# A prologue in a written order on three engines: filter network first, transposes of x later, and products of zeros in the gaps

## The chip, the cores and the metric

The kernel runs on one core of one Trainium2 chip. The metric is device time in microseconds from launch to end. Engine names are those of the profile: TensorE (PE; its weight loads PEld), VectorE (DVE), ScalarE (ACT), GpSimd (POOL), SyncE (SP, which here only issues loads).

## The reference

Two layers of a diffusion backbone over 512 tokens of 1024 channels, all in float32. Layer 0 mixes tokens with a Hyena long convolution beside neighbourhood attention, then a ConvFFN; layer 1 is a Conformer convolution and a ConvFFN. Only the start of layer 0 is touched. What it needs:

```python
shift1, scale1, ... = split(silu(c) @ w_mod[0] + b_mod[0])     # and the same for c_ctx
hn = rms_norm(x, g_mix_pre) * (1 + scale1) + shift1
...
def hyena_filters(length, w1, b1, w2, b2, w3, b3, w4, freq):
    ...
    hdn = jnp.sin(freq[0] * (z @ w1 + b1))          # z (512, 33) is a constant, hidden width 64
    hdn = jnp.sin(freq[1] * (hdn @ w2 + b2))
    hdn = jnp.sin(freq[2] * (hdn @ w3 + b3))
    filt = hdn @ w4                                  # (512, 1024)
    return filt[:, :512] * decay, filt[:, 512:] * decay
def bidirectional_fft_conv(v, h_fwd, h_bwd, bias):   # needs the spectrum of the two filters
    ...
```

## The kernel before

The large products of the kernel run on TensorE as three fp32r products of high and low halves: a high half is a cast by ScalarE (`A.copy`), the low half the difference by VectorE. Weights stream in through SP, are split in this way, and TensorE multiplies. Before the first product of the stream (tile `pz`, the input projection) there is a prologue, and the change is in it alone. Its parts:

- **The filter network.** `layer1`, `layer2` and `layer3` are small float32 products on TensorE (tiles `pf`), each followed by `sin_stage`: VectorE scales and range-reduces (tile `sx`: one to three instructions of L662, then L663 and L664), ScalarE takes the sine (L665; tiles `hdn`, `hdn`, then `h`). `w4x` holds w4 with a negated copy (ScalarE, L717), a decay step (GpSimd, L710) and a copy of that (ScalarE, L718).
- **The filters.** `filt("a")` and `filt("b")` multiply `h` by `w4x` in four float32 products each (L743, tiles `pf`), VectorE multiplies by the decay table (L745, `fx`), ScalarE casts the high half (L746, `fah`/`fbh`), VectorE takes the low half (L747, `fal`/`fbl`); at the end ScalarE makes negated copies (L750, `neg`).
- **The tables of the transform.** `tfr` comes by DMA; ScalarE casts it (L727, `TFh`), VectorE takes the low half (L728, `TFl`).
- **x.** For each of four chunks ScalarE sums squares (L408), GpSimd computes the reciprocal root (L401, L403), VectorE scales (L498, tile `junk`). `x_T(kc)` transposes one column block of all four chunks on TensorE (four products with the identity, L705, tile `pt`), and ScalarE copies it out (L706, `xT`).
- **The modulation.** `gemv_k(k, ...)` multiplies 32-column pieces of silu(c) with the loaded `w_mod` (L674, tile `g`, 16 loads `land`), `columns` brings the result into columns (tile `pm`), `modulate` makes the first operand `hT` out of `xT`.
- **The spectra.** `kspec(fc, pr, half)` is 12 products of a table with a filter for each half (tile `pk`): half 0 uses filter a, half 1 filter b.

The order is a string of step names. TensorE follows it; on the other engines the scheduler places the instructions. All tiles in PSUM come from one pool of eight buffers.

```python
    order_pe.enter_context(tc.manual_schedule(engines={mybir.EngineType.PE}))
    for key in "1 x0 x1 2 x2 x3 3 t0 t1 t2 t3 t4 t5 t6 t7 g0 a b g123 k00 k01 g4567 k100 c m k101 k11".split():
        steps[key[0]](*(int(i) for i in key[1:]))
```

SP issues the loads in the order of another string: four chunks of x, two of `tfr`, two of the decay table, 16 of `w_mod`, 512 KB each. The loads share eight queue semaphores, so each load of `w_mod` is issued when the load eight places ahead of it has landed.

Of the kernel before, what the change touches and what calls it, by code (L numbers as in the profile page):

```python
# [235 lines left out]
def backbone_kernel(ctx: ExitStack, tc: tile.TileContext, a, cols, out, dump=None, stop=None, mark=lambda s: None):  # L236
# [18 lines left out]
    def s4(dt=F32, shape=(P, 2, 512), n="s"):  # L255
        return spool.tile(list(shape), dt, name=nm(n), tag="s")
# [7 lines left out]
    def ps(n="ps"):  # L264
        return pspool.tile([P, 512], F32, name=nm(n), tag="ps")
# [10 lines left out]
    def f(ap):  # L276
        return ap.bitcast(F32)
# [35 lines left out]
    def flat(ap, pat):  # L313
        return ap.rearrange(pat)
# [178 lines left out]
    def norm_chunk(hc, halves=1):  # L493
        junk = s4(F32, (P, 1024), "junk")
        cut = [slice(i * (1024 // halves), (i + 1) * (1024 // halves)) for i in range(halves)]
        r = rstd([sumsq(hc[:, sl], junk[:, sl]) for sl in cut])
        for sl in cut:
            V.tensor_scalar(junk[:, sl], hc[:, sl], r, None, op0=ALU.mult)  # L498
        return junk
# [148 lines left out]
            SP.dma_start(r, a["wmod"][i % 2, i // 2])  # L648
            land[i] = r

    for key in "x0 x1 x2 x3 t0 t1 d0 d1 l0 l1 l2 l3 l4 l5 l6 l7 l8 l9 l10 l11 l12 l13 l14 l15".split():
        load_p(key)


# [3 lines left out]
    def sin_stage(src, i, dst, w):  # L658
        x_ = s4(F32, (P, 1024), "sx")
        v, k = x_[:, 0:w], x_[:, 512:512 + w]  # L660
        for s_, r, o in src:
            V.tensor_scalar(v[r, o], s_[r, o], pc("flt", i)[r], turn[r, i:i + 1], op0=ALU.add, op1=ALU.mult)  # L662
        V.tensor_scalar(k, v, MAGIC, None, op0=ALU.add)  # L663
        V.scalar_tensor_tensor(v, k, MAGIC, v, op0=ALU.subtract, op1=ALU.subtract)  # L664
        return A.activation(dst, v, AF.Sin, bias=0.0, scale=-2.0 * PI_F)  # L665
# [28 lines left out]
        sin_stage([(pm, slice(None), slice(0, 256))], 1, h2, 256)  # L694


    def x_norm(c):
        xns[c] = norm_chunk(xc[c])

    def x_T(kc):  # L700
        if kc % 2 == 0:
# [4 lines left out]
        A.copy(strip(xT[kc // 2][:, kc % 2]), nat(pt))  # L706


    def layer3():
        G.tensor_tensor(w4x[64:128, 0:512], w4x[64:128, 0:512], zt[64:128, 512:1024], op=ALU.mult)  # L710
        pm = [ps("pf") for _ in range(2)]
        for i, o, src, ro in ((0, slice(0, 256), slice(0, 256), 0), (1, slice(256, 512), slice(0, 256), 0),
                              (0, slice(0, 255), slice(1, 256), 64), (0, slice(255, 256), slice(255, 256), 64),
                              (1, slice(255, 511), slice(0, 256), 64), (1, slice(511, 512), slice(255, 256), 64)):
            rs = slice(64 * i, 64 * i + 64)
            PE.matmul(pm[i][ro:ro + 64, o], fl[rs, 128:192], h2[rs, src], start=True, stop=True)
        A.mul(w4x[0:64, 512:1024], w4x[0:64, 0:512], -1.0)  # L717
        A.copy(w4x[64:128, 512:1024], w4x[64:128, 0:512])  # L718
        h3s.append(s4(F32, (P, 1024), "h3"))
        sin3 = sin_stage([(pm[0], slice(None), slice(0, 256)), (pm[1], slice(None), slice(256, 512)),  # L720
                          (pm[1], slice(64, 128), slice(255, 256))], 2, h3s[0][:, 0:512], 512)
        G.memset(h3s[0][64:128, 511:512], 0.0)

        for i in range(2):
            hv = flat(TFh[i], "p a b -> p (a b)")
            with tc.issue_after(sin3.ins):
                A.copy(hv, tfr[i])  # L727
            V.tensor_tensor(flat(TFl[i], "p a b -> p (a b)"), tfr[i], f(hv), op=ALU.subtract)  # L728

    def tfs(lo, ch, cs, fc):  # L730
        t_ = (TFl if lo else TFh)[ch // 2]
# [4 lines left out]
    fb = [p8(n="fbh"), p8(n="fbl")]  # L736
    neg = {}

    def filt(key, dst, which):
        for ch in range(4):  # L740
            s0 = 256 * (ch % 2) + ch // 2
            pm = ps("pf")
            PE.matmul(pm, h3s[0][:, s0:s0 + 255:2], w4x[:, which * 512:(which + 1) * 512], start=True, stop=True)  # L743
            X = s4(F32, (P, 1024), "fx")[:, 0:512]
            V.tensor_tensor(X, pm, dec[ch // 2][:, ch % 2], op=ALU.mult)  # L745
            A.copy(dst[0][:, ch], X)  # L746
            V.tensor_tensor(dst[1][:, ch], X, f(dst[0][:, ch]), op=ALU.subtract)  # L747
        for lo in range(2):
            t_ = s4(F32R, n="neg")
            A.mul(t_, f(dst[lo][:, 2:4]), -1.0)  # L750
            neg[(key, lo)] = t_


    K = {}
# [52 lines left out]
    def modulate():  # L807
# [5 lines left out]
        for kc in range(8):  # L813
# [4 lines left out]
            if kc == 1:  # L818
                ws.splits(2)

    steps = {"1": layer1, "2": layer2, "3": layer3, "x": x_norm, "t": x_T, "g": gemv_k, "c": columns, "m": modulate,
             "a": lambda: filt("a", fa, 0), "b": lambda: filt("b", fb, 1), "k": kspec}
# [723 lines left out]
```

## Time and profile before

| | |
|---|---|
| median of 3 runs | 1267.14 us (1264.29 to 1267.49) |
| the profiled execution | 1264.98 us, its span 1263.2 us |
| PE busy | 1239.3 us (98%) |
| DVE busy | 815.2 us (65%) |
| ACT busy | 509.2 us (40%) |
| POOL busy | 89.4 us (7%) |
| mean granted TensorE clock | 0.999 |
| memory traffic | 134 GB/s over the span |

The profiled execution is one of the faster ones: the median lies 2.16 us above it. Span and time differ by 1.78 us, which lies outside the first and the last instruction. The end of a product is modelled in the profile, so a busy TensorE is not one at its peak: the distance between starts says more than the duration.

### The profile page before, as it was taken

What the parts mean: (1) busy time and instruction counts of PE and PEld (TensorE: products, weight loads), DVE (VectorE), ACT (ScalarE), POOL (GpSimd) and SP (SyncE); (2) the same over time, 40 slices, a digit from 0 to 9 for tenths busy, and PEclk for the clock granted to TensorE, in tenths of its full rate; (3) what the DMA queues carried; (4) which work ended last, traced back from release to release, by engine and by line L of the source; (5) the groups of instructions that cost most, each with busy time, mean ns of one, the idle gap of its engine ahead of it and who ended that gap; (6) DMA issues with size and microseconds to landing.
All of it is one profiled execution on the core that took longest, in us unless ns stands there. A gap on an engine that the chain in (4) does not pass through costs nothing.

```text
span 1263.2 us, 15493 instructions
## 1 busy us (share of the span) xinstructions
PE 1239.3 (98%) x6044; PEld 1024.2 (81%) x6044; DVE 815.2 (65%) x1072; ACT 509.2 (40%) x788; POOL 89.4 (7%) x157
## 2 busy tenths in 40 slices
PE   6999999999999999999999999999999999999997
PEld 3688888988898888887888887878988888888886
DVE  4577696876567788778534576686687555566233
ACT  5453333576443332336223442233544333344221
POOL 3110000231200000000000100012100000000001
PEclk9999999999999999999999999999999999999999
DMA  9535434743136577764344331120265233332321
GB/s 351 192 114 170 133 110 142 257 152 128 40 101 216 184 240 245 226 193 146 117 132 135 131 104 55 50 101 1 68 203 178 88 98 100 100 100 90 95 84 66
DMA packets 47865, 171.64 MB, mean 136 GB/s; under 512 B 5741, under 2 KB 5772, under 8 KB 47792
## 3 DMA queue, kind: packets, MB, share of 16 engines
q1 hardware_dynamic: 47428, 169.93, 41.4%
q8 instruction: 47, 0.77, 0.2%
q0 software_dynamic: 176, 0.40, 0.1%
q10 hardware_dynamic: 188, 0.33, 0.1%
q14 instruction: 26, 0.21, 0.1%
HBM read 167.76 MB, written 2.10 MB: 134 GB/s over the span
## 4 chain that ended last, share of the span: by engine, by line
PE 76%; DMA 9%; DVE 9%; ACT 2%; issue 2%; POOL 1%; DVEq 0%; POOLq 0%; ACTq 0%
PE pz L280 11%; PE pz L281 11%; PE pz L282 11%; PE acc L282 8%; PE acc L280 8%; PE acc L281 8%; DMA raw<-in_wup 4%; DMA raw<-in_wcol 4%; DVE w L298 3%; PE pg L280 2%; PE pg L282 2%; PE pg L281 2%; DVE acc L430 2%; DMA raw<-in_wgate 1%; ACT w L297 1%
## 5 line engine op out<-in xcount | busy, mean ns | idle before, releaser
L281 PE MATMUL pz<-hTl,w 128*128 128x512 f32 (+1 forms) x920 | 345.4, 376 | 0.0
L280 PE MATMUL pz<-hTh,w 128*128 128x512 f32 (+1 forms) x920 | 344.6, 377 | 0.5 <-DVE hTh L521 0.5
L282 PE MATMUL pz<-hTh,w 128*128 128x512 f32 (+1 forms) x920 | 345.1, 376 | 0.0
L298 DVE TENSOR_TENSOR w<-raw,w 128x1024 fp32r<-128x1024 f32 x159 | 193.9, 1222 | 199.9 <-ACT w L297 194.0
L297 ACT CAST w<-raw 128x1024 fp32r<-128x1024 f32 x159 | 166.4, 1051 | 331.8 <-PE pz L281 132.0
L282 PEld LDWEIGHTS pz<-hTh,w 128*128 128x128 f32 x920 | 173.8, 189 | 31.4
L281 PEld LDWEIGHTS pz<-hTl,w 128*128 128x128 f32 x920 | 173.8, 189 | 30.0 <-DVE hTl L522 0.4
L280 PEld LDWEIGHTS pz<-hTh,w 128*128 128x128 f32 x920 | 173.0, 189 | 31.0 <-DVE hTh L521 1.0
L430 DVE SCALAR_TENSOR_TENSOR acc<-raw,sc,acc 128x1024 f32<-128x1024 f32 x74 | 95.4, 1289 | 41.4 <-DMA raw<-in_wgate 20.8
L281 PE MATMUL acc<-w,gs 128*128 128x512 f32 x256 | 99.6, 389 | 0.0
L282 PE MATMUL acc<-w,gs 128*128 128x512 f32 x256 | 98.4, 390 | 0.5 <-DVE gs L1317 0.5
L280 PE MATMUL acc<-w,gs 128*128 128x512 f32 x256 | 97.0, 389 | 0.0
L879 ACT ACTIVATE cv<-pz,pk 128x512 f32<-128x512 f32 x88 | 67.6, 772 | 0.7 <-PE pz L282 0.7
L881 DVE SCALAR_TENSOR_TENSOR cv<-pz,pk,cv 128x511 f32<-128x511 f32 x88 | 65.6, 747 | 1.8
L880 DVE SCALAR_TENSOR_TENSOR cv<-pz,pk,cv 128x511 f32<-128x511 f32 x88 | 65.1, 744 | 0.2 <-ACT cv L879 0.2
L1279 ACT ACTIVATE cv<-cv 128x512 f32<-128x512 f32 x44 | 27.7, 629 | 81.6 <-DVE cv L881 81.5
L282 PEld LDWEIGHTS acc<-w,gs 128*128 128x128 f32 x256 | 48.0, 188 | 10.9 <-DVE gs L1317 0.9
L280 PEld LDWEIGHTS acc<-w,gs 128*128 128x128 f32 x256 | 48.1, 188 | 10.1 <-DVE cv L881 0.2
L281 PEld LDWEIGHTS acc<-w,gs 128*128 128x128 f32 x256 | 48.1, 188 | 9.9
L298 DVE TENSOR_TENSOR wk<-raw,wk 128x1024 fp32r<-128x1024 f32 x30 | 37.1, 1245 | 29.0 <-ACT wk L297 28.9
L536 DVE TENSOR_TENSOR py<-acc,gg 128x512 f32<-128x512 f32 x32 | 21.8, 688 | 49.1 <-ACT py L408 49.1
L399 POOL TENSOR_SCALAR t<-t,t 128x1 f32<-128x1 f32 x19 | 7.0, 369 | 636.6 <-ACT py L408 628.1
(327 smaller groups left out, 1934.5 us busy)
## 6 DMA issues: line engine op xcount, KB each, us to landing
raw<-in_wup SPq DMA_DIRECT2D x88, 512.0 KB, 3.6
raw<-in_wcol SPq DMA_DIRECT2D x48, 512.0 KB, 4.6
raw<-in_wdn SPq DMA_DIRECT2D x44, 512.0 KB, 3.6
raw<-in_wgate SPq DMA_DIRECT2D x32, 512.0 KB, 4.4
raw<-in_pw SPq DMA_DIRECT2D x24, 512.0 KB, 3.9
raw<-in_win SPq DMA_DIRECT2D x20, 512.0 KB, 3.5
land<-in_wmod SPq DMA_DIRECT2D x16, 512.0 KB, 10.4
BM<-in_rpb SPq DMA_DIRECT2D x8, 512.0 KB, 3.4
```

Of the source, the lines that this page charges most:

```text
L280: PE.matmul(o, ah, bh, start=start, stop=False)
L281: PE.matmul(o, ah, bl, start=False, stop=False)
L282: PE.matmul(o, al, bh, start=False, stop=stop)
L297: A.copy(hi, r)
L298: V.tensor_tensor(lo, r, f(hi), op=ALU.subtract)
L399: G.tensor_scalar(v, sums[0], sums[1], EPS, op0=ALU.add, op1=ALU.add)
L430: V.scalar_tensor_tensor(acc, rs[k], ck_, init if k == 0 else acc, op0=ALU.mult, op1=ALU.add)
L536: V.tensor_tensor(p_[:, sl], y2[i], gg[:, sl], op=ALU.mult)
L879: A.activation(dst, pz, AF.Identity, bias=pc(bk, i), scale=pc(wk + "1", i))
L880: V.scalar_tensor_tensor(dst[:, 1:w], pz[:, 0:w - 1], pc(wk + "0", i), dst[:, 1:w], op0=ALU.mult, op1=ALU.add)
L881: V.scalar_tensor_tensor(dst[:, 0:w - 1], pz[:, 1:w], pc(wk + "2", i), dst[:, 0:w - 1], op0=ALU.mult, op1=ALU.add)
L1279: A.activation(cv[:, 0], cv[:, 0], AF.Silu, bias=0.0, scale=1.0)
```

## The change

The scheduler no longer places the prologue's instructions on ScalarE and VectorE: up to the end of filter b, the three engines run in the order in which the code is written. The steps are cut into parts for that (sum and scale of x, product, high half and low half of a filter, high and low half of a table). The network comes first, then filter a, then the tables among the transposes of x, then filter b. The gemv of k = 0 is no longer alone: k = 0 to 3 go in one call. The decay table is loaded ahead of `tfr`. Twenty-three products of a 128x128 tile of zeros stand in the network's gaps on TensorE; nothing reads their result.

```diff
+    warm = cpool.tile([P, P], F32, name="warm")
+    V.memset(warm, 0.0)
+    warm_ps = pspool.tile([P, 512], F32, name="warm_ps", tag="ps")
+    def warm_up(n):
+        for _ in range(n):
+            PE.matmul(warm_ps[:, 0:P], warm, warm, start=True, stop=True)
...
-    for key in "x0 x1 x2 x3 t0 t1 d0 d1 l0 l1 ...".split():
+    for key in "x0 x1 x2 x3 d0 d1 t0 t1 l0 l1 ...".split():
...
-    def x_norm(c):
-        xns[c] = norm_chunk(xc[c])
+    def x_sum(c):
+        xns[c] = s4(F32, (P, 1024), "xn")
+        xns[c, "r"] = rstd([sumsq(xc[c], xns[c])])
+    def x_scale(c):
+        V.tensor_scalar(xns[c], xc[c], xns[c, "r"], None, op0=ALU.mult)
...
+    def filt(key, ch, part):
+        dst, which = (fa, 0) if key == "a" else (fb, 1)
+        if part == "p":
...
+            PE.matmul(fx[key, ch], h3s[0][:, s0:s0 + 255:2], w4x[:, which * 512:(which + 1) * 512], start=True, stop=True)
+        elif part == "m":
...
+            V.tensor_tensor(X, fx[key, ch], dec[ch // 2][:, ch % 2], op=ALU.mult)
+            A.copy(dst[0][:, ch], X)
...
+        else:
+            V.tensor_tensor(dst[1][:, ch], fx.pop((key, ch)), f(dst[0][:, ch]), op=ALU.subtract)
...
+    early.enter_context(tc.manual_schedule(engines={mybir.EngineType.PE, mybir.EngineType.Activation,
+                                                    mybir.EngineType.DVE}))
+    warm_up(5)
+    layer1()
+    warm_up(3)
+    w4_decay()
+    w4_neg()
+    x_sum(0)
+    layer2()
+    warm_up(5)
+    x_sum(1)
+    x_scale(0)
+    layer3(0)
+    warm_up(10)
+    w4_copy()
+    x_sum(2)
+    x_sum(3)
+    layer3(1)
+    for ch in range(4):
+        filt("a", ch, "p")
...
+    for i in range(2):
+        x_T(i)
+        table_hi(i)
+        table_lo(i)
+    for i in range(2, 4):
+        x_T(i)
+    for ch in range(4):
+        filt("b", ch, "p")
+        filt("b", ch, "m")
+        if ch:
+            filt("b", ch - 1, "l")
+    filt("b", 3, "l")
+    early.close()
...
-    for key in "1 x0 x1 2 x2 x3 3 t0 t1 t2 t3 t4 t5 t6 t7 g0 a b g123 k00 k01 g4567 k100 c m k101 k11".split():
-        steps[key[0]](*(int(i) for i in key[1:]))
+    kspec(0, 0, 0)
+    x_T(4)
+    x_T(5)
...
+    kspec(1, 0, 0)
+    x_T(6)
+    x_T(7)
...
+    kspec(0, 0, 1)
+    kspec(1, 0, 1)
+    gemv_k(0, 1, 2, 3)
+    gemv_k(4, 5, 6, 7)
+    kspec(0, 1, 0)
+    columns()
+    modulate()
+    kspec(0, 1, 1)
+    kspec(1, 1)
```

Lines of the changed kernel lie 9 to 92 further down than those of before. From the second filter's end on, every engine has the same instructions in the same order as before, except for the moved transposes and gemv on TensorE, the moved copies and negations of these parts on ScalarE, and one copy of `columns` on VectorE that trades places with its neighbour.

ScalarE before, in the network's stretch (`junk` out of `xc` is a chunk's sum of squares, `hdn` and `h` the sines):

```order
L717 ACTIVATE w4x_80<-w4x_80 64x512
L372 CAST onesr<-ones 128x128
L387 COPY SCT_117<-sc 128x8
L392 ACTIVATE SCT_117<-pk 128x8
L718 COPY w4x_80<-w4x_80 64x512
L665 ACTIVATE hdn_180<-sx_190 128x256
L408 ACTIVATE junk_195,t_196<-xc_84 128x1024
L408 ACTIVATE junk_203,t_204<-xc_85 128x1024
L408 ACTIVATE junk_219,t_220<-xc_86 128x1024
L665 ACTIVATE hdn_180<-sx_214 128x256
L408 ACTIVATE junk_227,t_228<-xc_87 128x1024
L665 ACTIVATE h_59_246<-sx_247 128x512
```

ScalarE in the changed kernel, from the copy for silu(c_ctx) on:

```order
L401 ACTIVATE SCT_120<-pk 128x8
L674 ACTIVATE hdn_183<-sx_198 128x256
L723 ACTIVATE w4x_83<-w4x_83 64x512
L417 ACTIVATE xn_208,t_209<-xc_87 128x1024
L674 ACTIVATE hdn_183<-sx_218 128x256
L417 ACTIVATE xn_228,t_229<-xc_88 128x1024
L729 COPY w4x_83<-w4x_83 64x512
L417 ACTIVATE xn_255,t_256<-xc_89 128x1024
L417 ACTIVATE xn_262,t_263<-xc_90 128x1024
L674 ACTIVATE h_59_269<-sx_270 128x512
```

The first sine has moved ahead of the two `w4x` instructions; the second and the third sine each have as many sums of x ahead of them as the rows show, the last one all four.

VectorE before, from the second sine's range reduction on (L498 scales a chunk of x):

```order
L662 TENSOR_SCALAR sx_214<-pf_211,pk,turn 128x256
L498 TENSOR_SCALAR junk_195<-xc_84,t_200 128x1024
L663 TENSOR_SCALAR sx_214<-sx_214 128x256
L664 SCALAR_TENSOR_TENSOR sx_214<-sx_214 128x256
L498 TENSOR_SCALAR junk_203<-xc_85,t_208 128x1024
L498 TENSOR_SCALAR junk_219<-xc_86,t_224 128x1024
L498 TENSOR_SCALAR junk_227<-xc_87,t_232 128x1024
L662 TENSOR_SCALAR sx_247<-pf_236,pk,turn 128x256
L662 TENSOR_SCALAR sx_247<-pf_237,pk,turn 128x256
L662 TENSOR_SCALAR sx_247<-pf_237,pk,turn 64x1
L663 TENSOR_SCALAR sx_247<-sx_247 128x512
L664 SCALAR_TENSOR_TENSOR sx_247<-sx_247 128x512
```

VectorE in the changed kernel, from the same place:

```order
L671 TENSOR_SCALAR sx_218<-pf_215,pk,turn 128x256
L672 TENSOR_SCALAR sx_218<-sx_218 128x256
L673 SCALAR_TENSOR_TENSOR sx_218<-sx_218 128x256
L711 TENSOR_SCALAR xn_208<-xc_87,t_213 128x1024
L671 TENSOR_SCALAR sx_270<-pf_236,pk,turn 128x256
L671 TENSOR_SCALAR sx_270<-pf_237,pk,turn 128x256
L671 TENSOR_SCALAR sx_270<-pf_237,pk,turn 64x1
L672 TENSOR_SCALAR sx_270<-sx_270 128x512
L673 SCALAR_TENSOR_TENSOR sx_270<-sx_270 128x512
L711 TENSOR_SCALAR xn_228<-xc_88,t_233 128x1024
L711 TENSOR_SCALAR xn_255<-xc_89,t_260 128x1024
L774 TENSOR_TENSOR fx_288<-pf_278,dec_139 128x512
```

Of the four scales of x that stood ahead of the third sine's instructions, one is left; the others follow them, two ahead of the first filter product's `fx`.

TensorE before, from the last transposes on (`g` is the gemv of k = 0, `pf` filter a):

```order
L705 MATMUL pt_305<-ident,junk_219 128x128
L705 MATMUL pt_305<-ident,junk_227 128x128
L674 MATMUL g_311<-land_146,SCT_117 32x512
L674 MATMUL g_313<-land_146,SCT_117 32x512
L674 MATMUL g_315<-land_148,SCT_117 32x512
L674 MATMUL g_317<-land_148,SCT_117 32x512
L743 MATMUL pf_319<-w4x_80,h_59_246 128x512
L743 MATMUL pf_325<-w4x_80,h_59_246 128x512
L743 MATMUL pf_331<-w4x_80,h_59_246 128x512
L743 MATMUL pf_337<-w4x_80,h_59_246 128x512
```

TensorE in the changed kernel, after the third layer, and then the start of the gemv:

```order
L355 MATMUL warm_ps<-warm 128x128 x10
L771 MATMUL pf_278<-w4x_83,h_59_269 128x512
L771 MATMUL pf_280<-w4x_83,h_59_269 128x512
L771 MATMUL pf_282<-w4x_83,h_59_269 128x512
L771 MATMUL pf_284<-w4x_83,h_59_269 128x512
L718 MATMUL pt_306<-ident,xn_208 128x128
L718 MATMUL pt_306<-ident,xn_228 128x128
L718 MATMUL pt_306<-ident,xn_255 128x128
L718 MATMUL pt_306<-ident,xn_262 128x128
```

```order
L683 MATMUL g_460<-land_149,SCT_120 32x512
L683 MATMUL g_460<-land_153,SCT_120 32x512
L683 MATMUL g_460<-land_157,SCT_120 32x512
L683 MATMUL g_460<-land_161,SCT_120 32x512
L683 MATMUL g_465<-land_149,SCT_120 32x512
L683 MATMUL g_465<-land_153,SCT_120 32x512
```

Filter a now comes ahead of the transposes (16 of 32 follow it, the others stand between spectra), and the gemv goes through four different loads, k = 0 to 3, for each of its four results.

## Rows read from the trace of the kernel before

**Rows 1.** Busy time by stretch, TensorE: microseconds, PE busy (records), PEclk, DMA share, GB/s.

```profile
0.00:16.59 16.59, 4.58 (x24) 1.00 0.88 295
...
36.17:47.27 11.10, 11.10 (x51) 1.00 0.11 45
...
63.64:1255.00 1191.36, 1185.84 (x5794) 1.00 0.40 129
```

**Rows 2.** Chain that ended last, first 64 us: start, microseconds, what.

```profile
8.03 0.61 ACT w4x L718
8.67 0.42 ACT hdn L665
...
15.78 0.76 DVE junk L498
16.59 5.46 PE pt L705 x29
22.05 3.55 PE g L674 x8
25.60 7.07 PE pf L743 x16
32.67 3.56 PE g L674 x24
...
47.34 3.57 PE g L674 x32
...
53.86 1.75 PE pm L792 x16
...
63.80 0.26 PE pz L280
```

**Rows 3.** VectorE in order of time: start, microseconds, instruction.

```profile
5.23 0.54 DVE L662 TENSOR_SCALAR sx<-pf,pk,turn 128x256 f32<-128x256 f32 x1
...
6.14 0.43 DVE L664 SCALAR_TENSOR_TENSOR sx<-sx 128x256 f32<-128x256 f32 x1
10.33 0.55 DVE L662 TENSOR_SCALAR sx<-pf,pk,turn 128x256 f32<-128x256 f32 x1 [3.77 <-PE pf L693]
11.22 0.75 DVE L498 TENSOR_SCALAR junk<-xc,t 128x1024 f32<-128x1024 f32 x1 [0.34 <-POOL t L403]
...
16.45 1.31 DVE L662 TENSOR_SCALAR sx<-pf,pk,turn 128x256 f32<-128x256 f32 x3
...
18.25 0.69 DVE L664 SCALAR_TENSOR_TENSOR sx<-sx 128x512 f32<-128x512 f32 x1
```

**Rows 4.** TensorE in order of time, the network's second and third layer.

```profile
9.14 1.12 PE L693 MATMUL pf<-hdn,fl 64*64 64x256 f32 x4 [5.05 <-ACT hdn L665]
13.16 1.25 PE L716 MATMUL pf<-hdn,fl 64*64 64x256 f32 x12 [2.91 <-ACT hdn L665]
```

**Rows 5.** Busy time of transposes alone in a stretch: PE, PEld, DVE, ACT, PEclk, DMA, GB/s.

```profile
16.58:20.69 4.11, 4.10 (x19) 4.11 (x20) 0.00 (x0) 0.24 (x1) 1.00 1.02 417
```

**Rows 6.** SP in order of time, two stretches: issues that wait for x.

```profile
8.53 0.55 SPq L648 DMA_DIRECT2D land<-in_wmod  x1
...
12.58 0.33 SPq L648 DMA_DIRECT2D land<-in_wmod  x1
```

**Rows 7.** Groups of ScalarE by form, 0 to 45 us: count, busy, mean ns.

```profile
L408 ACT ACTIVATE junk<-xc 128x1024 f32<-128x1024 f32 x4 | 4.2, 1044 | 0.0
L706 ACT COPY xT<-pt 128x512 f32<-128x512 f32 x8 | 4.1, 612 | 0.0
L746 ACT CAST fah<-fx 128x512 fp32r<-128x512 f32 x4 | 2.5, 619 | 3.4 <-DVE fx L745 3.4
...
L727 ACT CAST TFh<-tfr 128x1024 fp32r<-128x1024 f32 x2 | 2.1, 1052 | 0.0
...
L665 ACT ACTIVATE h<-sx 128x512 f32<-128x512 f32 x1 | 0.6, 630 | 4.8 <-DVE sx L664 4.8
```

**Rows 8.** Group of VectorE by form, 0 to 45 us: the tables' low halves.

```profile
L728 DVE TENSOR_TENSOR TFl<-tfr,TFh 128x1024 fp32r<-128x1024 f32 x2 | 2.5, 1225 | 3.3 <-ACT TFh L727 3.3
```

More of the change, by code (lines that the diff above doesn't have):

```diff
@@ L649, in load_p @@
             land[i] = r
[L651 removed]
+    for key in "x0 x1 x2 x3 d0 d1 t0 t1 l0 l1 l2 l3 l4 l5 l6 l7 l8 l9 l10 l11 l12 l13 l14 l15".split():
         load_p(key)
@@ L706, in x_T, with w4_neg, w4_decay, w4_copy @@
         A.copy(strip(xT[kc // 2][:, kc % 2]), nat(pt))
-    def layer3():
+    def w4_neg():
+        A.mul(w4x[0:64, 512:1024], w4x[0:64, 0:512], -1.0)
+    def w4_decay():
         G.tensor_tensor(w4x[64:128, 0:512], w4x[64:128, 0:512], zt[64:128, 512:1024], op=ALU.mult)
[L711 to L717, printed above, removed]
-        A.copy(w4x[64:128, 512:1024], w4x[64:128, 0:512])
+    def w4_copy():
+        A.copy(w4x[64:128, 512:1024], w4x[64:128, 0:512])
@@ new lines, in layer3 @@
+    def layer3(part):
+        if part == 0:
+            pm = [ps("pf") for _ in range(2)]
+            h3s.append(pm)
+            for i, o, src, ro in ((0, slice(0, 256), slice(0, 256), 0), (1, slice(256, 512), slice(0, 256), 0),
+                                  (0, slice(0, 255), slice(1, 256), 64), (0, slice(255, 256), slice(255, 256), 64),
+                                  (1, slice(255, 511), slice(0, 256), 64), (1, slice(511, 512), slice(255, 256), 64)):
+                rs = slice(64 * i, 64 * i + 64)
+                PE.matmul(pm[i][ro:ro + 64, o], fl[rs, 128:192], h2[rs, src], start=True, stop=True)
+            return
+        pm = h3s.pop()
@@ L719, in layer3, with table_hi @@
         h3s.append(s4(F32, (P, 1024), "h3"))
-        sin3 = sin_stage([(pm[0], slice(None), slice(0, 256)), (pm[1], slice(None), slice(256, 512)),
-                          (pm[1], slice(64, 128), slice(255, 256))], 2, h3s[0][:, 0:512], 512)
+        sin_stage([(pm[0], slice(None), slice(0, 256)), (pm[1], slice(None), slice(256, 512)),
+                   (pm[1], slice(64, 128), slice(255, 256))], 2, h3s[0][:, 0:512], 512)
         G.memset(h3s[0][64:128, 511:512], 0.0)
[L724 to L728, printed above, removed]
+    def table_hi(i):
+        A.copy(flat(TFh[i], "p a b -> p (a b)"), tfr[i])
@@ L730, in tfs, with table_lo @@
+    def table_lo(i):
+        V.tensor_tensor(flat(TFl[i], "p a b -> p (a b)"), tfr[i], f(flat(TFh[i], "p a b -> p (a b)")), op=ALU.subtract)
     def tfs(lo, ch, cs, fc):
@@ L819, in modulate @@
                 ws.splits(2)
[L821 to L822 removed]
+    early = ExitStack()
+    early.enter_context(tc.manual_schedule(engines={mybir.EngineType.PE, mybir.EngineType.Activation,
[18 more added lines that the diff above has]
+        filt("a", ch, "p")
+    x_scale(1)
+    x_scale(2)
+    filt("a", 0, "m")
+    filt("a", 1, "m")
+    x_scale(3)
+    filt("a", 0, "l")
+    for ch in (2, 3):
+        filt("a", ch, "m")
+        filt("a", ch - 1, "l")
+    filt("a", 3, "l")
+    for i in range(2):
[11 more added lines that the diff above has]
+    early.close()
     order_pe = ExitStack()
     order_pe.enter_context(tc.manual_schedule(engines={mybir.EngineType.PE}))
[L825 to L826 removed]
+    kspec(0, 0, 0)
+    x_T(4)
+    x_T(5)
+    for lo in range(2):
+        negate("a", lo)
+    kspec(1, 0, 0)
+    x_T(6)
+    x_T(7)
+    for lo in range(2):
+        negate("b", lo)
+    kspec(0, 0, 1)
[7 more added lines that the diff above has]
+    kspec(1, 1)
     order_pe.close()
```

17 lines of the change are left out of this document (7 added, 10 removed).

## Prediction

> **What bounds the kernel now.** First the busy time by stretch: from 63.64 to 1255 us TensorE works 1185.84 of 1191.36 us, before 16.59 us it works only 4.58 [rows 1]. So TensorE bounds everything behind the prologue, and since the order there does not change, that part should move as one block: what the prologue gives, the end gives. Then the chain of waits of the first 64 us [rows 2]. It has two parts. Up to 16.59 it lies on ScalarE, GpSimd and VectorE: the first sine (8.67) waits in ScalarE's queue behind the copy into `w4x` (8.03), and at the end the last scale of x (15.78) releases the transposes. From 16.59 on it lies on TensorE alone, without a gap, to the first product of the stream at 63.80: 29 transposes 5.46, gemv of k = 0 3.55, filters 7.07, gemv of k = 1 to 3 3.56, four half spectra (36.23 to 47.34) 11.11, gemv of k = 4 to 7 3.57, a half spectrum 2.95, `columns` 1.75, three half spectra 8.19; together 47.2. So three things can move the end: when TensorE's unbroken work starts, what it contains, and how fast it runs.
>
> As to how fast: the granted-clock column says 1.00 from the start, also where TensorE has not begun, so I go by the pace. Between 16.58 and 20.69 us 19 transposes took 4.10 us, 0.216 each [rows 5]; the 16 of `columns` took 1.75, 0.109 each [rows 2]. That is the ratio of the lower level (1.2 GHz) to the upper (2.4 GHz). 29 at 0.109 are 3.16, with a switch of about 0.2 to the gemv 3.36: about 2.1 us of the 5.46 is the lower level. It ended near 20.8, while TensorE did nothing but transposes: the ten left after 20.69 fit into 1.3 us.
>
> **The change, step by step: when filter a can start.** The first sine's range reduction stays at 5.23 to 6.57 [rows 3]. The sine no longer stands behind the `w4x` copy, so it runs at 6.6 instead of 8.67 and takes 0.42 [rows 2]. The second layer follows at 7.1; VectorE got its result 1.19 after its start [rows 3, 4], so 8.3. The range reduction took 1.34 the first time; the second time, from 10.33, a scale of x (11.22, 0.75) stood in the middle [rows 3]. That scale now comes later, so it ends at 9.65. ScalarE does the sum of chunk 0 ahead of the second sine. x0 had landed by 8.53 (SP's issue of the first `w_mod` load waits for it) [rows 6], a sum takes 1.04 [rows 7], so it is done at about 9.65 too, and the sine ends at 10.1. Third layer from 10.15 to 11.4 [rows 4]. VectorE does one scale in front: chunk 0's sum starts at 8.55 instead of behind the first sine (8.67 + 0.42), 0.55 earlier, so its scale runs from 10.7 to 11.45 instead of 11.22; then the third range reduction, 16.45 to 18.94 before, 2.49 [rows 3]: 11.65 to 14.15. ScalarE meanwhile does three sums and a copy, 3 x 1.04 + 0.61 from 10.1, to 13.85; x3 has landed by 12.58 [rows 6], which leaves the last sum at 12.8 to 13.85. Third sine 0.63 [rows 7]: to 14.8. Filter a at 14.9, where before the filters started at 25.60 and the unbroken work at 16.59.
>
> **What it contains then.** The same pieces by the same rows: filters 7.07, 32 transposes at 0.109 = 3.49, two gemv calls of 3.57, half spectra 11.11 + 2.95 + 8.19, `columns` 1.75: 41.7 us. The gemv of k = 0 alone costs no less than one of three or of four values of k (8, 24 and 32 records in 3.55, 3.56 and 3.57 [rows 2]): the 32-column pieces run beside each other. Two calls of four instead of one, three and four are 3.55 less. All 32 transposes are inside now, where three had run before 16.59, which costs 0.33. There are about four more switches between kinds of work; by the 0.1 to 0.2 that a switch costs in these rows, 0.5. 14.9 + 41.7 + 0.5 = 57.1.
>
> **Does VectorE and ScalarE's part arrive in time?** Filter a's first result reaches VectorE about 1.2 later (as in the second layer [rows 3, 4]): 16.1. From there the two engines alternate over four chunks; with fx and low half at 0.6 to 0.7 (half of the 1.23 of a low half of twice the size [rows 8]), a scale of 0.75 [rows 3] and casts of 0.62 [rows 7], the last low half of filter a is done at 22.2. ScalarE copies a transposed block, casts a table, copies, casts: 0.51 (4.1 for eight) + 1.05 twice [rows 7], from 21.5 to 24.6. VectorE's low halves of the tables take 1.23 each [rows 8]: 23.1 to 24.35 and 24.65 to 25.9. TensorE does filter a to 18.5, four transpose blocks to 20.3, filter b to 23.9, and the first half spectrum wants the first low table at 24.5 and the second at 25.85. That is 0.05 late, on the edge: each microsecond that this alternation takes longer is one that TensorE waits. The eight PSUM buffers go round in order, and filter b's third and fourth product wait for `fx` of chunks 2 and 3 (19.6 and 20.9, wanted at 22.1 and 23.0). Filter b's last low half comes at 33.0, behind two negations that I put at a table cast's 1.05 each; it is wanted at 33.9. All `w_mod` is on the chip by about 37.5: in 36.17 to 47.27 the DMA engines are busy for 0.11 of 11.1 us [rows 1]; the second gemv call would start at 40.1. `modulate` keeps its distance to `columns`, and of the loads behind x3, which land 1.35 apart ((12.58 - 8.53) / 3 [rows 6]), the decay halves come at 13.9 and 15.3, wanted at 16.1 and 19, the tables at 16.6 and 18.0, wanted at 22. I add 0.1: 57.2.
>
> **The products of zeros.** A float32 product is two records; at 128 columns it costs twice a transpose, 0.43 at the lower level, 0.22 at the upper, by rows 5 and 2. Five ahead of the first layer (2.2) end when its data lands, near 3, and VectorE starts at 5.23 anyway. Three fit into the gap before 7.1. Five behind the second layer end at 10.4 at the lower level: third layer 0.2 late. Ten behind the third layer end at 13.8 at the upper, 15.9 at the lower level, against 14.9: 0 to 1.0 late. With layer 2 and the zeros TensorE works unbroken from 7.1 on, and unbroken work came ahead of the rise before; I take the level as up during the ten, so nothing for the zeros, and 1.2 as the bound.
>
> So 63.8 becomes 57.2: a gain of 6.6 us (1.7 earlier start, 3.55 gemv, 2.0 transposes, less 0.6). The sum is made against the profiled execution: 1264.98 - 6.6 = 1258.4; against the median, 1260.5. I give the middle, **1259.4 us**. A change under 0.3%, 3.8 us, is about what a measurement of this kernel cannot tell from none.
>
> In this execution the lower level held until about 20.7 [rows 5], which is 2.1 us of the sum. The Trainium skill (TensorE: Matmul & The Clock Gate, Part 1, "What's actually happening") says of such a ramp that it differs from run to run and warns against fitting to one count. By that rule another execution of the kernel before may have paid less, and the gain against it would be as low as 4.5; by the row it is 6.6. One execution cannot show which.
>
> **Rivals.** *The level rises late.* It may stay down through the zeros and rise only under filter a. Then the ten zeros run to 15.9, and filter a starts there; a record costs 0.88 instead of 0.44 (7.07 / 16) until the rise. None to all eight records so are 0 to 3.5 us; I take five, 2.2, with the late start 3.2. Gain 3.4: 1261.6 on the profiled time, 1262.6 in the middle. For it: layers 1 to 3 did not lift the level before; but they were four microseconds apart (9.14 and 13.16 [rows 4]). *The alternation is slower.* Some ten hand-overs between VectorE and ScalarE lie between 16.1 and 25.9; at 0.1 to 0.2 us more each, TensorE waits 1 to 2 us at the first spectrum: gain 5.1, 1260.9 in the middle. For it: the margin is nil; against: where they alternated before, the rows already hold it. *Slower than before:* the lower level lasts through filters, transposes and first spectra, between which TensorE now changes eight times. Each microsecond of it costs a half, so 6.6 is used up when the low level lasts 13.2 us past 14.9, to 28.1, and the kernel is 0.3% slower when it lasts to 36 (1269 to 1270). Against it: it rose before while the same transposes ran [rows 2, 5]. *The gain is given back later:* no load or engine after 63.64 waits for a fixed moment; TensorE's 5.5 us of idle there are waits for VectorE and ScalarE that move along.
>
> **How the numbers follow.** Forecast 0.64 (its own range 1257 to 1261.5), late level 0.15, slower alternation 0.14, slower than before 0.04, given back 0.03. Faster by over 0.3%: the forecast, the alternation and a third of the late level, 0.64 + 0.13 + 0.05 = 0.82; within: 0.14; slower: 0.04. Range: 1256 if the start falls with the fastest runs (1264.29 - 6.6 = 1257.7, less 1.2 for a faster network at the upper level), to 1263.5, the late level on a slower run.
>
> **What would show it.** Right: first sine near 6.6, third near 14.2; filter a at about 14.9; one gemv of 32 records where two stood; transposes at 0.109; first `pz` near 57. Wrong: transposes or filter products at twice their pace; a wait of TensorE on `TFl` of over 0.5 us; a sine that waits for a sum; `pz` at the old distance from `columns` no longer kept.

## The result, and the profile after

The changed kernel takes 1259.41 us (median of 7 runs, 1257.72 to 1260.61), the kernel before beside it 1266.87 us (7 runs, 1262.99 to 1270.05): a ratio of 0.9947 with a 95% interval of 0.9929 to 0.9965, so it is faster by 0.5%. The forecast was 1259.4 us. The profiled execution of the changed kernel took 1260.43 us, its span 1258.6 us.

The chain that ended last, first 64 us, of the changed kernel (start, microseconds, what):

```profile
4.14 4.87 DMA xc<-in_x
9.04 1.15 ACT xn L417 x2
10.19 0.30 ACT hdn L674
...
13.88 1.27 POOL t L412
15.21 3.68 PE pf L771 x8
18.89 1.75 PE pt L718 x16
20.64 3.44 PE pf L771 x8
...
26.98 0.87 PE pt L718 x8
30.61 0.88 PE pt L718 x8
36.97 7.00 PE g L683 x64
46.92 1.75 PE pm L824 x16
56.84 0.26 PE pz L280
```

These rows answer to [rows 2]. TensorE's unbroken part begins at 15.21 (before 16.59) and is 41.63 long (before 47.21): 16 transposes now take 1.75 and two pieces of eight 0.87 and 0.88, where 29 took 5.46 in one piece, and one piece of 64 `g` products takes 7.00 where three took 10.68 together. The first `pz` stands at 56.84 where it stood at 63.80: 6.96 earlier.

TensorE in order of time, the same stretch (in brackets the idle time before, and what ended it):

```profile
6.64 1.43 PE L702 MATMUL pf<-hdn,fl 64*64 64x256 f32 x4 [0.47 <-ACT hdn L674]
8.00 2.50 PE L355 MATMUL warm_ps<-warm 128*128 128x128 f32 x10
10.54 1.25 PE L740 MATMUL pf<-hdn,fl 64*64 64x256 f32 x12
11.73 2.96 PE L355 MATMUL warm_ps<-warm 128*128 128x128 f32 x20
15.21 3.68 PE L771 MATMUL pf<-w4x,h 128*128 128x512 f32 x8 [0.52 <-POOL t L412]
18.73 1.91 PE L718 MATMUL pt<-ident,xn 128*128 128x128 f32 x16
```

The last group of zeros ends before filter a's operand is there; TensorE then waits 0.52. (The profile puts this down to GpSimd's `t`; ScalarE's sine `h` ends at 15.11, below, and that is what the product reads.) The level of the clock is read from the pace, here by stretch for `warm_ps` alone (PE busy and records, PEld, PEclk, DMA share, GB/s):

```profile
11.73:12.66 0.93, 0.93 (x4) 0.93 (x5) 1.00 1.04 401
12.80:14.40 1.60, 1.60 (x16) 1.60 (x16) 1.00 1.01 369
```

Four records in 0.93, then sixteen in 1.60. The edges of the stretches blur this; the starts of the records lie 0.21 apart up to 12.74 and 0.11 from there on, so the second pace is about twice the first. The trace's own record of the granted clock, which the views do not print step by step, has the rise to the upper level at 12.73 us, within the ten zeros; before, it stood at 20.89, within the transposes. As before, the column prints 1.00 for both stretches.

ScalarE and VectorE in order of time, changed kernel:

```profile
6.17 0.42 ACT L674 ACTIVATE hdn<-sx 128x256 f32<-128x256 f32 x1 [0.81 <-DVE sx L673]
9.04 1.06 ACT L417 ACTIVATE xn<-xc 128x1024 f32<-128x1024 f32 x1 [1.93 <-DMA xc<-in_x]
10.09 0.40 ACT L674 ACTIVATE hdn<-sx 128x256 f32<-128x256 f32 x1
...
14.48 0.63 ACT L674 ACTIVATE h<-sx 128x512 f32<-128x512 f32 x1
```

```profile
13.76 0.69 DVE L673 SCALAR_TENSOR_TENSOR sx<-sx 128x512 f32<-128x512 f32 x1
...
24.51 1.22 DVE L753 TENSOR_TENSOR TFl<-tfr,TFh 128x1024 fp32r<-128x1024 f32 x1 [0.21 <-ACT TFh L750]
```

The first sine no longer stands behind the copy into `w4x` (6.17 instead of 8.67), the second waits for chunk 0's sum, which itself waited 1.93 for the load, the third runs at 14.48. The second low half of the tables is done at 25.73.

### The profile page after: what moved, and what is told of

The parts are those of the page before. It is cut to its first block, busy times and chain, and to the rows that moved or that the text cites. A ratio compares the mean times of both kernels' runs of the same rounds, so it can differ in the third digit from the quotient of the medians.

```text
span 1258.6 us, 15586 instructions
## 1 busy us (share of the span) xinstructions
PE 1243.5 (99%) x6090; PEld 1029.6 (82%) x6090; DVE 815.7 (65%) x1073; ACT 508.7 (40%) x788; POOL 89.2 (7%) x157
## 4 chain that ended last, share of the span: by engine, by line
PE 91%; DVE 3%; DMA 2%; ACT 2%; issue 1%; POOL 0%; SPq 0%; DVEq 0%; POOLq 0%; ACTq 0%
PE pz L280 15%; PE pz L281 15%; PE pz L282 15%; PE acc L282 8%; PE acc L280 8%; PE acc L281 8%; PE pg L280 2%; PE pg L281 2%; PE pg L282 2%; DMA raw<-in_wcol 1%; PE po L1266 1%; PE pt L1246 1%; PE va L280 1%; PE va L281 1%; PE va L282 1%
```

## The experiments

Eleven more kernels were run: ten edits, and the changed kernel a second time. One theory was on trial in all of them: the end moves by as much as the first `pz`, and that is set by the network's start, the contents of TensorE's queue, and the level of the clock. The rivals were that the written order itself is worth nothing (the gemv alone explains it), and that the zeros do nothing.

### Without the products of zeros

```diff
-        for _ in range(n):
+        for _ in range(0):
             PE.matmul(warm_ps[:, 0:P], warm, warm, start=True, stop=True)
```

> The changed kernel without its 23 products of zeros; the output is unaffected. If the zeros are what brings TensorE to its upper level ahead of filter a (in the changed kernel the pace doubled at 12.7 us, inside the ten zeros), then filter a starts at about 15.2 as before but at 0.86 a record instead of 0.43 for most of its eight records, the rise comes inside the filters or the transposes, and the first product of the stream moves from 56.7 to between 58.5 and 60; time 2 to 3.3 us longer. If the level rises by itself with the network's layers, the first product stays at 56.3 to 56.8 and the time is the same.

Measured: 0.9962 of before (0.9952 to 0.9972), first `pz` 59.37 (start of its first record; 56.68 in the change, 63.64 before). TensorE in order of time:

```profile
10.74 1.25 PE L740 MATMUL pf<-hdn,fl 64*64 64x256 f32 x12 [2.74 <-ACT hdn L674]
15.41 6.33 PE L771 MATMUL pf<-w4x,h 128*128 128x512 f32 x8 [3.41 <-POOL t L412]
21.58 1.91 PE L718 MATMUL pt<-ident,xn 128*128 128x128 f32 x16
```

Filter a starts only 0.20 later than in the change (x0 landed that much later: its sum starts at 9.24 instead of 9.04), but its eight records take 6.33 instead of 3.68. The rise is recorded at 20.77, inside filter a. So in this pair of traces the zeros are worth 2.7 us of `pz`, by the level: the one row of filter a has 2.65 of it. The times of the two overlap; the trace is what shows it. It is one pair, and the rise moves from trace to trace: against the next experiment, where it comes at 16.33, the zeros are worth about 1.5 (59.37 - (59.64 - 1.74)), with x0 0.34 later there than here.

### The gemv in three calls again

```diff
-    gemv_k(0, 1, 2, 3)
+    gemv_k(0)
+    gemv_k(1, 2, 3)
```

> The changed kernel with the gemv of k = 0 alone again, then k = 1 to 3, then k = 4 to 7: the work of before in the changed order. If the calls cost by their loads beside each other and not by their number of k, one more call is 3.55 us of TensorE with nothing beside it, and the first product of the stream goes from 56.7 to 60.2, the time up by 3.5. If the gemv of k = 0 is a filler that hides in a wait, or if modulation is waited for anyway, the first product stays within 0.5 us of 56.7.

Measured: 0.9964 (0.9951 to 0.9978), `pz` 59.64. The chain of this kernel, and below it TensorE in order of time:

```profile
38.18 8.74 PE g L683 x64
```

```profile
12.27 4.42 PE L355 MATMUL warm_ps<-warm 128*128 128x128 f32 x20
16.52 3.60 PE L771 MATMUL pf<-w4x,h 128*128 128x512 f32 x8
```

The expectation missed: 1.74 more than 7.00, not 3.5. The starts of the records show why. `gemv_k(0)` has eight records in one 32-column place; four start one after another, 0.43 apart, and the other four each together with three of the next call. In the kernel before, where filter a stood behind it, the same call took its full 3.55. The remaining 1.2 of `pz` is no matter of the gemv: here the rise is recorded at 16.33, the ten zeros last 4.42 instead of 2.96 and filter a starts at 16.52. Up to there the program is the change's own, so this is also a further execution of its start.

### Before, with k = 0 to 3 in one call

```diff
-    for key in "1 x0 x1 2 x2 x3 3 t0 t1 t2 t3 t4 t5 t6 t7 g0 a b g123 k00 k01 g4567 k100 c m k101 k11".split():
+    for key in "1 x0 x1 2 x2 x3 3 t0 t1 t2 t3 t4 t5 t6 t7 a b g0123 k00 k01 g4567 k100 c m k101 k11".split():
```

> The kernel before with only the gemv changed: k = 0 to 3 in one call behind the filters. The sum says 3.55 us less between the transposes and the first spectrum, the first product of the stream from 63.6 to 60.1, the time 3.5 us down, half of the whole gain. The rival, in which the gemv of k = 0 covered a wait for the filter network (its sine was done at 19.6, the transposes at 22), says 63.6, no change.

Measured: 0.9978 (0.9968 to 0.9987), `pz` 60.03, 3.61 earlier than before. In the chain one piece of 32 records stands where 8 and 24 stood:

```profile
29.07 3.57 PE g L674 x32
```

This one edit, without any written order on the other engines, gives half of the move of `pz`: the 3.55 of the prediction.

### Before, with products of zeros

```diff
-    for key in "1 x0 x1 2 x2 x3 3 t0 t1 t2 t3 t4 t5 t6 t7 g0 a b g123 k00 k01 g4567 k100 c m k101 k11".split():
+    for key in "1 w10 x0 x1 2 w6 x2 x3 3 w6 t0 t1 t2 t3 t4 t5 t6 t7 g0 a b g123 k00 k01 g4567 k100 c m k101 k11".split():
```

> The kernel before with 22 products of zeros in TensorE's gaps (ten behind the first layer, six behind the second, six behind the third). If the lower level in the transposes cost 2.1 us, the 29 transposes from 16.6 on now go at 0.109 from the start and the first product of the stream comes at 61.5 instead of 63.6; the six behind the third layer may delay the first three transposes without harm. If zeros do not lift the level, transposes stay at 0.216 until about 20.8 and the first product at 63.6. In time, 2 us or nothing.

Measured: 0.9999 (0.9989 to 1.001), `pz` 62.02. TensorE in order of time:

```profile
4.02 3.94 PE L354 MATMUL warm_ps<-warm 128*128 128x128 f32 x20
8.92 0.65 PE L701 MATMUL pf<-hdn,fl 64*64 64x256 f32 x4 [0.97 <-ACT hdn L673]
...
12.94 0.74 PE L724 MATMUL pf<-hdn,fl 64*64 64x256 f32 x12 [1.84 <-ACT hdn L673]
13.61 2.71 PE L354 MATMUL warm_ps<-warm 128*128 128x128 f32 x12
```

The level rose at 7.06, during the first zeros (`w10` is ten of them), but TensorE then idled for 1.0 and 1.8 us ahead of the second and third layer, the level fell at 13.89, during the last zeros, and rose again at 17.30, during the transposes. `pz` gained 1.62, and the time shows none of it. That the waits left between the zeros are why the level fell is the likely reading; no run tests it.

### The order written for TensorE alone

```diff
-    early.enter_context(tc.manual_schedule(engines={mybir.EngineType.PE, mybir.EngineType.Activation,
-                                                    mybir.EngineType.DVE}))
+    early.enter_context(tc.manual_schedule(engines={mybir.EngineType.PE}))
```

> The changed kernel with the written order on TensorE alone; ScalarE and VectorE are placed by the scheduler again. If the written order on those two is what brings filter a to 15.2 us (sines not behind sums and scales of x), the third sine is late again, filter a starts at 17 to 20 and the first product of the stream comes at 58.5 to 61.5. If the order on TensorE alone does it (network and filters ahead of the transposes), it stays at 56.5 to 57.5, or 58 with a late rise of the clock.

Measured: 1.0065 (1.0045 to 1.0086), slower than before, `pz` 71.52. The size was far off: 14.8 us later than in the change. ScalarE in order of time:

```profile
8.07 0.61 ACT L729 COPY w4x<-w4x 64x512 f32<-64x512 f32 x1 [1.10 <-POOL w4x L726]
17.84 1.04 ACT L750 CAST TFh<-tfr 128x1024 fp32r<-128x1024 f32 x1 [9.15 <-DMA tfr<-in_tf]
18.79 0.41 ACT L674 ACTIVATE hdn<-sx 128x256 f32<-128x256 f32 x1
```

The scheduler put the cast of a table ahead of the first sine. ScalarE waits 9.15 us for the table's load while `sx` has been ready since 6.3; the whole network stands behind it, and the third sine runs at 29.45.

This is not the scheduling of the kernel before. There the casts were tied behind the third sine by one line, which the change dropped:

```diff
-        for i in range(2):
-            hv = flat(TFh[i], "p a b -> p (a b)")
-            with tc.issue_after(sin3.ins):
-                A.copy(hv, tfr[i])
...
+    def table_hi(i):
+        A.copy(flat(TFh[i], "p a b -> p (a b)"), tfr[i])
```

ScalarE before, in order of time:

```profile
18.98 0.63 ACT L665 ACTIVATE h<-sx 128x512 f32<-128x512 f32 x1 [4.83 <-DVE sx L664]
19.52 1.03 ACT L727 CAST TFh<-tfr 128x1024 fp32r<-128x1024 f32 x1
```

So the 14.8 us are the price of giving up the written order without putting that line back. What the scheduler would do in the changed kernel with the line was not run.

### The order written for TensorE and ScalarE

```diff
-    early.enter_context(tc.manual_schedule(engines={mybir.EngineType.PE, mybir.EngineType.Activation,
-                                                    mybir.EngineType.DVE}))
+    early.enter_context(tc.manual_schedule(engines={mybir.EngineType.PE, mybir.EngineType.Activation}))
```

> TensorE and ScalarE in the written order, VectorE in the scheduler's. If ScalarE's queue alone made the kernel with both engines left to the scheduler slow (its first sine stood behind a cast of a table, which waited for the table to land), this one costs only what VectorE's rows cost: the scale of chunk 1 ahead of the third range reduction and those of chunks 2 and 3 in the midst of it, 0.75 us each, and the wait of chunk 3's scale for its sum: third sine 1 to 2.5 us later than in the change, pz 57.8 to 59.3, time 1260 to 1262. If VectorE's order is as costly as ScalarE's, pz is past 62 and the time 1265 or more.

Measured: 0.9987 (0.9974 to 1.0), `pz` 61.69. ScalarE's order was indeed what cost most in the experiment above, but `pz` is 2.4 past the upper end of what was expected, and the time, 1264.3 us, 2.3 past it. TensorE in order of time, and below it by stretch over all engines (span, then PE, PEld, DVE, ACT, POOL, PEclk, DMA share, GB/s):

```profile
11.35 2.50 PE L355 MATMUL warm_ps<-warm 128*128 128x128 f32 x20
17.75 5.28 PE L771 MATMUL pf<-w4x,h 128*128 128x512 f32 x8 [3.90 <-issue]
...
30.80 0.50 PE L282 MATMUL pk<-fah,TFl 128*128 128x512 f32 x1 [0.76 <-DVE TFl L753]
```

```profile
17.75:20.90 3.15, 3.15 (x4) 1.48 (x5) 0.69 (x1) 0.34 (x1) 0.09 (x1) 0.50 1.03 421
21.10:22.80 1.70, 1.70 (x5) 0.73 (x4) 1.59 (x3) 0.34 (x2) 0.00 (x0) 1.00 1.02 412
```

The third sine came 2.54 later (17.02), at the upper end of what was expected: three scales of x stood ahead of it on VectorE. But the zeros had ended, TensorE idled 3.90 us, and the level, up since 10.75, fell at 17.58. The column shows it here: 0.50, then 1.00 from 20.99 on. Filter a's eight records took 5.28, 1.60 more than in the change, and then a table's low half, which VectorE had put behind three `fx`, was 0.76 late. 2.54 + 1.60 + 0.76 are 4.90 of the 5.01 by which `pz` is later. This is the lower level of the prediction's rivals, reached by a late operand.

### The transposes ahead of filter a

```diff
+    for i in range(8):
+        x_T(i)
...
     for ch in range(4):
         filt("a", ch, "p")
```

> The changed kernel with all 32 transposes ahead of filter a, and the three scales of x ahead of filter a's VectorE work; all else as in the change. By the sum nothing but the start of unbroken work changes: it waits for the scale of the last chunk, 16.7 instead of 15.2, so the first product of the stream comes 1.5 later, 58.2. The rival, that filters first is what lets VectorE and ScalarE finish in time, says that TensorE then also waits for the filters' halves or the tables at the first spectrum, 59.5 or later.

Measured: 0.9963 (0.9951 to 0.9975), `pz` 59.05, 2.37 later than in the change. TensorE in order of time:

```profile
15.98 0.38 PE L718 MATMUL pt<-ident,xn 128*128 128x128 f32 x2
16.64 0.33 PE L718 MATMUL pt<-ident,xn 128*128 128x128 f32 x1 [0.27 <-DVE xn L711]
18.15 3.39 PE L718 MATMUL pt<-ident,xn 128*128 128x128 f32 x29 [1.19 <-DVE xn L711]
```

(The edit also puts the scales of x and the casts and low halves of the tables ahead of filter a's work on VectorE and ScalarE; TensorE has no wait for them in this trace.) The fourth transpose needs the last chunk, whose sum, root and scale end at 18.1; filter a needs only the third sine, which ends at 15.75 here. TensorE's unbroken part starts 2.94 later, with 0.33 of transposes already done. The expectation, 58.2, missed by 0.85, and most of that is no matter of the order: x0's sum starts at 9.68 here, 0.64 later than in the change, because the load landed later. About 1.7 of the 2.37 are left for the order. So the network ahead of x counts beside the gemv and the level; the trace shows it, while the interval of the time overlaps that of the change.

### Ten of the twenty-three zeros

```diff
-    warm_up(5)
     layer1()
-    warm_up(3)
...
     layer2()
-    warm_up(5)
```

> The changed kernel with only the ten zeros behind the third layer; the thirteen ahead of it are left out. If the early ones matter, the upper level comes later than at 12.7 or 16.3 us (the two starts seen with all zeros), the ten run at the lower level to about 16.1, and filter a starts 0.9 later and partly at half pace: first product of the stream at 58 to 59.5. If the ten alone are enough, it comes at 56.5 to 58, as with all of them.

Measured: 0.9968 (0.9954 to 0.9982), `pz` 56.82. The rise is recorded at 13.85 instead of 12.73, still within the ten zeros, and `pz` is the change's to 0.14:

```profile
11.86 3.43 PE L355 MATMUL warm_ps<-warm 128*128 128x128 f32 x20
```

The ten last 0.47 longer than in the change, and filter a follows them at 15.35 without a wait. So the thirteen zeros ahead of the third layer gain nothing in this trace. Whether they bring the rise forward it cannot say: in two traces with all of them (11.20 in the second one of the change, 10.75 with TensorE and ScalarE in order) the level rose in the third layer, before the first of the ten.

### The sums of x later, two versions

The first (four zeros follow the second layer instead of five, and the scale of chunk 0 goes behind filter a's products):

```diff
-    x_sum(0)
     layer2()
+    x_sum(0)
     x_sum(1)
...
     x_sum(2)
-    x_sum(3)
     layer3(1)
+    x_sum(3)
```

> The changed kernel with the sum of chunk 0 behind the second sine, the sum of chunk 3 behind the third sine, the scale of chunk 0 behind the third range reduction, and one zero less. In the changed kernel's trace the second sine waited 0.65 us for the sum of x0. If that is what sets filter a, the second sine comes at 9.5 instead of 10.1, filter a at 14.4 instead of 15.2, the first product of the stream at 55.9 instead of 56.7. If VectorE's alternation up to the tables is the bound, the first spectrum waits longer and the first product stays at 56.5 or later. In time the difference to the change, 0.8, is too small to measure.

The second, on top of that (the scale of chunk 2 also goes between the first two `fx`):

```diff
-    x_sum(2)
     layer3(1)
+    x_sum(2)
     x_sum(3)
```

> The change with the sums of chunks 0 and 1 behind the second sine and those of 2 and 3 behind the third, and the scales of chunks 2 and 3 between the first filter products. If the sums of x on ScalarE are what holds the network back, the third sine runs at 13.4 and filter a starts at 14.1, 1.1 earlier than in the change. If the alternation of VectorE and ScalarE is then the bound, the second low half of the tables is still ready at 25 to 26 us and TensorE waits for it 0.5 to 1.2: pz 55.9 to 56.6, time as the change within 0.1%. If it isn't, pz is 55.5 and less.

Measured: 0.994 (0.9922 to 0.9959), `pz` 56.64, and 0.9947 (0.993 to 0.9965), `pz` 56.79. In the first, VectorE's part of the network was done at 13.5, but the third sine waited for chunk 2's sum until 14.25 (filter a at 14.96). In the second it did not (13.68); TensorE in order of time:

```profile
14.40 3.68 PE L771 MATMUL pf<-w4x,h 128*128 128x512 f32 x8 [0.56 <-issue]
...
18.75 1.64 PE L718 MATMUL pt<-ident,xn 128*128 128x128 f32 x13 [0.33 <-DVE xn L711]
...
24.49 0.50 PE L282 MATMUL pk<-fah,TFl 128*128 128x512 f32 x1 [0.20 <-DVE TFl L753]
```

Filter a starts 0.81 earlier than in the change and `pz` 0.11 later. VectorE's second low half runs from 24.64 to 25.87 here, no earlier than in the change (24.51 to 25.73): the alternation of the two engines over filter a, the scales of x and the tables is the next bound. Neither version can be told from the change by its time; the first has the lowest ratio of all that ran.

### The change once more

The same file, for a second trace.

> The changed kernel once more, for a second profile of the same program. The theory that the level's rise is no fixed moment: in the profile that is known the level rose at 12.73 us, in others with the same ten zeros between 11.53 and 16.33; here it should come somewhere from 11.5 to 16.5, and the first pz between 56.6 and 57.6. The theory that the stalls behind the prologue (near 237 and 519 us, 3 us in all) come from this change: they would stand here at the same places, and pz to the end would be 1201.9 again. The theory that they are loads that land differently from run to run: pz to the end between 1199 and 1202, with stalls elsewhere.

Measured: 0.9956 (0.9938 to 0.9975), `pz` 56.25, the rise at 11.20, 0.35 and 0.3 ahead of the expected ranges. Filter a started at 14.77 (15.21 in the first trace): x0's sum began at 8.25 instead of 9.04. The part behind the first `pz` took 1201.0, with the stalls of the first trace at the same places; what that says stands in the last point below.

## Why the prediction was right, step by step

**The total.** At `pz` 6.96 us were gained where 6.6 were forecast: the start gave 1.38 (1.7), the gemv 3.68 (3.55), the transposes 1.96 (2.0), and the 0.6 put down for switches and a late table cost about nothing. The terms hold, and `pz` keeps its distance from `columns` (9.92; 9.94 before). That the median came out at the forecast to 0.01 us is luck: the medians of the kernel before alone lie between 1264.22 and 1266.87 in the four series, and in the profiled pair the time fell by 4.55 us, not by 6.6.

**Filter a at 14.9.** It came at 15.21. The first sine was earlier than thought (6.17, not 6.6: the constants had landed sooner), but the second was done at 10.49, not 10.1, because x0 landed at 9.04. The bound of 8.53 came from [rows 6], a wait for the same load in another execution. 0.3 of the 1.7 was lost so. In the second trace of the same kernel x0's sum began at 8.25 and filter a at 14.77, so the forecast lies between the two; the landing of x0 moves this term by half a microsecond. A sine that waits for a sum was named as a sign of being wrong, and the second sine did wait, 0.65 (its `sx` was ready at 9.44): the prediction had both ready at 9.65, with nothing to spare.

**What TensorE's queue contains.** 41.7 and 0.5 for switches were forecast, 41.63 measured: filters 7.12, transposes 3.50, gemv 7.00, `columns` 1.75. The switches cost next to nothing. The gemv term (3.55) measured 3.68 in the change and 3.61 alone, with the order of before. What failed is its reason in general form, that a call of one k costs no less than one of four: with another call right behind it, half of it is hidden (1.74 instead of 3.5).

**The transposes, 2.0.** 16 in 1.75 is the upper level's pace, and 32 take 1.96 less than the 29 did. The prediction took the level as up during the ten zeros; it rose at 12.73 and 11.20 in the two traces of this kernel. But the sum gave the zeros no term, only a cost, and they are why this step held: without them it was 2.7 less. The rival of the late level did not come in the two traces of the change, but the same start came near it in the experiment with three calls: with a rise at 16.33 the ten zeros held TensorE for 4.42 and filter a started 1.3 later, where the bound was 1.2 (0.5 of it, though, is that the zeros themselves began later, behind a later x0). The Trainium skill (TensorE: Matmul & The Clock Gate, Part 1, "What's actually happening") says that the ramp differs from run to run; the traces agree for the kernels with zeros: the same start of the program rose at 11.20, 12.73 and 16.33 in three executions, and over all eight traces in which ten zeros follow a third layer near 10 or 11 us the rise lies between 10.75 and 16.33. For the kernel before, the doubt that was drawn from it, a gain as low as 4.5, is not borne out by the two traces there are: in those with neither zeros nor an early filter (before, and before with two calls) the rise lies at 20.89 and 20.95.

**The alternation on the edge.** The second low half of the tables was forecast for 25.9 and wanted at 25.85; it came at 25.73, and the first spectra show about 0.15 of waiting. That this margin is nil fits with what the second version of the later sums showed: an earlier sine gave nothing.

**Slower than before.** The mechanism exists and has now been seen: with TensorE and ScalarE in order, TensorE idled 3.90 us ahead of filter a, fell to the lower level and paid 1.60. In the change the idle time there is 0.52. The price is smaller than the rival needed, since the level was back 3.4 us later.

**The rest moves as one block.** The first `pz` and the times, all against before:

| kernel | first `pz` | ratio of times |
|---|---|---|
| the change | -6.96 us | 0.9947 (0.9929 to 0.9965) |
| the change once more | -7.39 | 0.9956 (0.9938 to 0.9975) |
| sums later, first version | -7.00 | 0.994 (0.9922 to 0.9959) |
| sums later, second version | -6.85 | 0.9947 (0.993 to 0.9965) |
| ten zeros | -6.82 | 0.9968 (0.9954 to 0.9982) |
| transposes first | -4.59 | 0.9963 (0.9951 to 0.9975) |
| no zeros | -4.27 | 0.9962 (0.9952 to 0.9972) |
| gemv in three calls | -4.00 | 0.9964 (0.9951 to 0.9978) |
| before, gemv in two calls | -3.61 | 0.9978 (0.9968 to 0.9987) |
| TensorE and ScalarE in order | -1.95 | 0.9987 (0.9974 to 1.0) |
| before, with zeros | -1.62 | 0.9999 (0.9989 to 1.001) |
| TensorE alone in order | +7.88 | 1.0065 (1.0045 to 1.0086) |

Divided by 1265 us, the move of `pz` lies inside the interval in ten of twelve rows (not for ten zeros, where the time gained less, nor, by a hair, for before with zeros). Between medians it was 7.46 us in the first series and 5.60 in the series of the last three kernels. So in the times the block does move, as far as intervals of 2.4 to 5.2 us in width can tell. In the profiled pair it does so only in part: of 6.96 at `pz`, 4.6 are left at the end. Busy time of all engines by stretch, changed kernel, to be held against the last of [rows 1]:

```profile
56.68:1248.00 1191.32, 1184.62 (x5783) 988.13 (x5782) 780.40 (x1012) 475.13 (x729) 71.72 (x119) 1.00 0.41 129
```

6.70 idle instead of 5.52, which is half of the 2.4 that are missing; the rest lies in records that end later. Followed record by record, TensorE is 6.84 us ahead of before up to 238 us, loses 2.0 between 238 and 250 and 2.0 more between 500 and 540, and wins back 1.7 behind that. The waits that are new, by the view of waits behind 60 us (waited for, total, times, longest):

```profile
PE pz L282 <- DVE w L298: 1.0, 2, 0.5
PE sc L1219 <- ACT PT L1254: 1.0, 1, 1.0
```

Ahead of `PT` the chain runs through loads of the modulation's weights in columns, whose sums on VectorE stand ahead of the attention's `P`, as in this row of it:

```profile
228.55 3.84 DMA raw<-in_wcol
```

The first of these loads are issued 6.9 us earlier than before, so they do move along; by 209 us they have lost 1.5 of it. A lag near 243 us, against before, stands in all twelve other traces, with `pz` early or late (0.3 to 2.7 us), so the trace of before is the one that had least of it. From `pz` to the end the traces take 1198.9 to 1202.0; the five with `pz` earliest average 1201.2, the other eight 1200.2. That some of the gain, up to about 1 us, is given back in these loads because TensorE comes earlier is not excluded; it is not shown either. This stays open.

**What gave how much.** Before with the gemv alone moves `pz` by 3.61, the change without zeros (gemv and written order) by 4.27, the change by 6.96; zeros without the written order gave 1.62. So by these traces the written order without the zeros is worth some 0.7 us of `pz`, not much more than the 0.44 by which filter a's start differs between two traces of the same kernel; with it the zeros give 2.7 instead of 1.62. The rival that the gemv alone explains the change is refuted for order and zeros together, hardly for the order alone. One part of the change was not tried by itself: the decay table's load ahead of `tfr`.

## What to carry to other kernels

Where a prologue ends in one unbroken queue on the bounding engine, ask for that queue's start, its contents and its clock, in that order, and count small calls by what stands right behind them. An engine that works through its queue in order, as ScalarE did here with the sine's operand ready, must not have an instruction that waits for a late load ahead of a critical chain: here one cast cost 9.15 us of waiting, and either the written order or the one line of the kernel before, which tied the cast behind the sine, prevented it. And when one engine's part is pulled forward, look at once for the next one on the edge: 0.8 us of earlier start gave nothing here.

## What the runs showed of the hardware that was not expected

- Products of zeros, whose result nobody reads, lift TensorE's level as others do: in the changed kernel and its variants with 10 to 23 of them the rise came between 10.75 and 16.33 us (27.61 where the network itself came 13 us late), without them at 20.77; in the two traces of before's order without zeros it came at 20.89 and 20.95.
- The level fell with the engine idle from 13.85 to 17.75, 3.90 us (fall at 17.58, before the next product at 17.75), and also, in the kernel before with zeros, at 13.89 within a group of zeros, after idle stretches of 1.0 and 1.8 us with work between.
- The granted-clock column prints 1.00 up to the first recorded step although the pace is the lower level's; after a step it is right (0.50 from 17.75 to 20.90).
- Products with 32-column weights in different places of the array start together, four at a time, 0.43 apart, also across two calls.
